# Feed-forward units of a hybrid decoder step: another order of factors and banks, and `down`'s low parts on GpSimd

## The chip, the cores and the metric

The kernel runs on one core of a Trainium2 chip. The time is device microseconds of that core, from one execution of the whole program; three runs of the kernel before are given by their median. Engines are named as in the profile: PE (TensorE, matmuls), PEld (its weight loads), DVE (VectorE), ACT (ScalarE), POOL (GpSimd), SP (SyncE, which only issues DMAs here).

## The reference, cut to what matters

One decoder layer for 1024 prompt tokens and 8 decode tokens (T = 1032 columns), model width 1024: a half-step feed-forward block, a mixer (windowed attention beside a Mamba-2 scan), cross attention, and a second half-step feed-forward block. The change touches the two feed-forward blocks:

```python
def swiglu(x, w_gate, w_up, w_down):
    return (jax.nn.silu(x @ w_gate) * (x @ w_up)) @ w_down
...
    x = x + (0.5 * swiglu(rms_norm(x, g_ffn1), w1_gate, w1_up, w1_down)).astype(x.dtype)
...
    x = x + (0.5 * swiglu(rms_norm(x, g_ffn2), w2_gate, w2_up, w2_down)).astype(x.dtype)
```

w_gate and w_up are 1024 x 2816, w_down is 2816 x 1024, all float32.

## The kernel before, in words

**Precision.** A float32 number is split into a high part (a cast to fp32r on ScalarE) and a low part (the difference, by a subtraction on DVE or GpSimd). A product is three matmuls: high x high, high x low, low x high (`three`, L328). Weights are split as they arrive by `split` (L315), which sends the low part to DVE and GpSimd in turn (L320); its high part is the cast at L319. Activations are split by `put` (cast L264, subtraction L265).

**Seven products for eight.** A unit works on 128 rows of the hidden width. The 1032 tokens are cut into P0 (388), P1 (388) and the rest R (256). For P0 and P1 a 2 x 2 block product is done in the Strassen-Winograd way: four weight matrices A11, A12, A21, A22 and four sums of them, S1 to S4 (`add_up`, the sum itself at L366), times the activation factors B11, B21, B22, T1 to T4, seven products in all, accumulated in three PSUM banks b1, b2, b3. The rest R is an ordinary product with the four A matrices, in a fourth bank.

**Units and pairs.** `gate_up(m)` loads 512 KB of gate and 512 KB of up weights (`raw_`, L325, two raw buffers for all units), makes the matrices, runs the products against the normalized x, and writes the hidden block with its own factors (`put`). Two `gate_up` units are followed by one `down`, which loads two blocks of 512 KB of w_down and adds its products to x (L501 to L518). There are 11 pairs in each block; the last `down` is `down_last`, an ordinary product. In unit 0 (`late`) the rest products come after all others.

**Banks.** Two sets of four PSUM banks are taken in turn by units; `down` runs twice (c = 0, 1) and uses both sets each time. In both kinds of unit b1 holds A11 x B11, a ScalarE copy seeds b2 from b1 (L399 in `gate_up`, L499 in `down`), and further products are accumulated on b2. Order of products in `gate_up`: A11, S2, A12, S3, S1, S4, A22, A21 (rest only). In `down`: A11, A21 (rest only), S1, S2, A12, S3, S4, A22.

**Weights in SBUF.** Split matrices live in four buffers (`fw`), raw weights in two (`fraw`), the sums in one tile (`fs`). Copies out of PSUM live in the ring `ts` of three buffers.

**Order.** The source order is a preference: the scheduler of the framework, which runs a timeline of its own, writes each engine's queue, and an engine then works through its queue in order. `mid1`, called after every `gate_up` of the first block, issues on SP a copy of 576 KB into u_scr for m = 4, 6, ..., 18, placed behind the load that `st["load"]` names at that time (L802).

Of the kernel before, what the change touches and what calls it, by code (L numbers as in the profile page):

```python
# [76 lines left out]
def tile_step(ctx, tc, a, o):  # L77
# [263 lines left out]
    def ffn(x, F, wg, wu, wd, fin, turn, mid=None):  # L341
# [27 lines left out]
        def gate_up(m):  # L369
            q = m % 2  # L370
            g_, u_ = raw_(cols_of(wg, m * 128)), raw_(cols_of(wu, m * 128))
            t = {"A11": g_[:, :512], "A12": g_[:, 512:], "A21": u_[:, :512], "A22": u_[:, 512:]}
            bk, rb = bank_set()
            b1, b2, b3 = bk
            sums = sums_of(m)
            e = {}

            def mat(name):
                if name == "S2":
                    add_up("S1", t, sums[:, :512])  # L380
                if name in SUMS and name not in t:
                    add_up(name, t, sums[:, :512] if name == "S3" else sums[:, 512:1024])
                return split(two(512), t[name])

            def rest(name, w):
                i = name in ("A21", "A22")
                first, last = name in ("A11", "A22"), name in ("A12", "A21")
                for j in range(4):
                    three(rb[:, int(i)], w, j, F["R"][j + (4 if name in ("A12", "A22") else 0)], first and j == 0, last and j == 3)

            def rest_end():
                gr, hr = u1_(NR), u1_(NR)
                nc.scalar.activation(gr, rb[:, 0], AF.Silu)
                nc.vector.scalar_tensor_tensor(hr, rb[:, 1], 0.5, gr, op0=OP.mult, op1=OP.mult)
                put(Hd["R"][q], hr, nc.vector)

            def evac(name):
                if name == "A11":
                    nc.scalar.copy(b2, b1)  # L399
                elif name == "S2":  # L400
                    e["U2"] = acc_(PA)
                    nc.scalar.copy(e["U2"], b2)
                elif name == "A12":
                    e["g0"] = g1_(PA)
                    nc.scalar.activation(e["g0"], b1, AF.Silu)
                elif name == "S3":
                    e["U3"] = acc_(PA)
                    nc.scalar.copy(e["U3"], b2)  # L408
                elif name == "S1":
                    e["u1"] = sq_(PA)  # L410
                    nc.vector.tensor_add(e["u1"], b3, e["U3"])  # L411
                elif name == "S4":
                    g1, u1 = g1_(PA), e["u1"]
                    nc.vector.tensor_add(g1, b3, e["U2"])
                    nc.scalar.activation(g1, g1, AF.Silu)
                    nc.vector.scalar_tensor_tensor(u1, u1, 0.5, g1, op0=OP.mult, op1=OP.mult)
                    if Hd["plain"]:
                        put(Hd["B22" if q else "B12"], u1, nc.vector)
                    elif q:
                        b12, t1 = Hd["b"]  # L420
# [1374 lines left out]
```

## Time and profile before

| | us |
|---|---|
| three runs, median (lowest, highest) | 2684.96 (2679.42, 2686.81) |
| profiled execution | 2680.7 |
| its span, first to last instruction | 2678.6 |
| PE busy | 2508.9 |
| DVE busy | 1806.0 |
| ACT busy | 1172.3 |
| POOL busy | 906.3 |

The first feed-forward block runs from about 105 to 831 us, the second from about 1940 to the end. An engine's busy time is the union of its instructions; a releaser is what an engine was waiting for when it stood idle, written as engine, tile and line.

### The profile page before, as it was taken

To read this page: it belongs to the slowest core of one execution; us is meant where nothing else is said; L and a number is where in the kernel's file an instruction comes from. 1 tells how busy PE (TensorE), PEld (TensorE's weight loads), DVE (VectorE), ACT (ScalarE), POOL (GpSimd) and SP (SyncE) were. 2 spreads that over 40 slices of the span, in tenths; PEclk is the share of its full clock that TensorE was granted. 3 is DMA by queue.
4 is the path that set the end of the run, shared out by engine and by line. 5 is a ranking of instruction groups with operands and counts; after the bars stand their busy time and mean duration, and the time that the engine had idled before them with its cause. 6 is when DMAs were issued, how large, how long until landed. Compare 5 with 4: busy or idle time off the path is not lost.

```text
span 2678.6 us, 42139 instructions
## 1 busy us (share of the span) xinstructions
PE 2508.9 (94%) x15999; PEld 2384.3 (89%) x15999; DVE 1806.0 (67%) x3660; ACT 1172.3 (44%) x2415; POOL 906.3 (34%) x675
## 2 busy tenths in 40 slices
PE   6899999999999999999797899989699999999998
PEld 5899999999998899999576899978689999999997
DVE  8566666666656777778568877564876666666665
ACT  5443333333334455554467623333343333333345
POOL 5433333333334111115156564102443333333333
PEclk9999999999999999999898999999899999999999
DMA  5411111111113222327657634573011111111112
GB/s 172 135 50 64 57 57 58 61 59 57 57 48 112 81 70 65 92 75 239 201 167 221 221 108 132 169 236 104 23 48 48 48 48 49 55 48 52 51 48 80
DMA packets 273747, 252.12 MB, mean 94 GB/s; under 512 B 17392, under 2 KB 243880, under 8 KB 273536
## 3 DMA queue, kind: packets, MB, share of 16 engines
q1 hardware_dynamic: 271872, 249.34, 30.2%
q8 instruction: 126, 2.06, 0.3%
q14 instruction: 77, 0.63, 0.1%
q10 hardware_dynamic: 1672, 0.09, 0.0%
HBM read 204.25 MB, written 49.98 MB: 95 GB/s over the span
## 4 chain that ended last, share of the span: by engine, by line
PE 70%; DVE 15%; DMA 7%; issue 3%; ACT 3%; POOL 1%; SPq 0%; DVEq 0%; ACTq 0%; POOLq 0%
PE fb L332 44%; PE pqkv L245 5%; PE pxbc L245 4%; PE pcq L245 3%; DMA fraw<-in_w_up_dram 2%; PE pco L245 2%; PE pwa L245 1%; DVE fs L366 1%; PE pwo L245 1%; PE po L1071 1%; PE ps L1045 1%; PE ptr L1065 1%; PE pd L245 1%; PE pzz L245 1%; PE cps L1604 1%
## 5 line engine op out<-in xcount | busy, mean ns | idle before, releaser
L235 POOL TENSOR_TENSOR wl<-wr,wh 128x1024 fp32r<-128x1024 f32 (+4 forms) x79 | 166.1, 2103 | 562.1 <-ACT wh L231 537.2
L320 POOL TENSOR_TENSOR fw<-fraw,fw 128x512 fp32r<-128x512 f32 x131 | 174.2, 1330 | 465.8 <-ACT fw L319 392.4
L320 POOL TENSOR_TENSOR fw<-fs,fw 128x512 fp32r<-128x512 f32 x128 | 172.3, 1346 | 400.4 <-ACT fw L319 347.2
L319 ACT CAST fw<-fs 128x512 fp32r<-128x512 f32 x256 | 158.2, 618 | 268.5 <-PE fb L332 152.5
L319 ACT CAST fw<-fraw 128x512 fp32r<-128x512 f32 x262 | 162.2, 619 | 189.6 <-PE fb L332 185.9
L366 DVE TENSOR_TENSOR fs<-fraw 128x512 f32<-128x512 f32 (+1 forms) x168 | 101.0, 601 | 141.7 <-DMA fraw<-in_w_up_dram 67.0
L320 DVE TENSOR_TENSOR fw<-fraw,fw 128x512 fp32r<-128x512 f32 x131 | 102.5, 782 | 110.9 <-ACT fw L319 110.6
L320 DVE TENSOR_TENSOR fw<-fs,fw 128x512 fp32r<-128x512 f32 x128 | 95.5, 746 | 99.1 <-ACT fw L319 99.1
L332 PE MATMUL fb<-hRh,fw 128*128 128x256 f32 x640 | 137.3, 280 | 0.5
L231 ACT CAST wh<-wr 128x1024 fp32r<-128x1024 f32 (+1 forms) x80 | 76.8, 960 | 99.4 <-PE pqkv L245 23.4
L332 PEld LDWEIGHTS fb<-hRh,fw 128*128 128x128 f32 x640 | 109.2, 188 | 3.7 <-DVE x L516 3.7
L245 PE MATMUL pxbc<-xh,wh 128*128 128x344 f32 x288 | 94.0, 326 | 2.0 <-DVE xr L882 2.0
L245 PE MATMUL pqkv<-xh,wh 128*128 128x344 f32 x288 | 94.0, 326 | 0.4 <-DVE x L546 0.3
L245 PE MATMUL pxbc<-xl,wh 128*128 128x344 f32 x288 | 93.5, 324 | 0.0
L245 PE MATMUL pqkv<-xh,wl 128*128 128x344 f32 x288 | 93.1, 323 | 0.0
L245 PE MATMUL pqkv<-xl,wh 128*128 128x344 f32 x288 | 93.0, 323 | 0.0
L245 PE MATMUL pxbc<-xh,wl 128*128 128x344 f32 x288 | 92.9, 323 | 0.0
L332 PE MATMUL fb<-hRl,fw 128*128 128x256 f32 x320 | 87.6, 278 | 0.0
L411 DVE TENSOR_TENSOR tu<-fb,ts 128x388 f32<-128x388 f32 x44 | 24.7, 562 | 90.3 <-ACT ts L408 90.3
L1052 ACT ACTIVATE pr<-pr,nm 128x128 f32<-128x128 f32 (+3 forms) x64 | 49.7, 776 | 53.7 <-DVE nm L1050 53.3
L332 PE MATMUL fb<-T2h,fw 128*128 128x388 f32 x160 | 53.8, 357 | 17.1 <-ACT fb L499 17.1
L245 PE MATMUL pzz<-xh,wh 128*128 128x344 f32 x192 | 64.3, 335 | 4.1 <-DVE tv L914 2.2
(798 smaller groups left out, 9395.8 us busy)
## 6 DMA issues: line engine op xcount, KB each, us to landing
fraw<-in_w_gate_dram SPq DMA_DIRECT2D x44, 512.0 KB
fraw<-in_w_up_dram SPq DMA_DIRECT2D x44, 512.0 KB
fraw<-in_w_down_dram SPq DMA_DIRECT2D x44, 512.0 KB
wr<-in_w_in_dram SPq DMA_DIRECT2D x32, 512.0 KB
x_scr<-x SPq DMA_DIRECT2D x16, 516.0 KB
x<-x_scr SPq DMA_DIRECT2D x16, 516.0 KB
bc<-acs_scr SPq DMA_DIRECT2D x16, 512.0 KB
ckv<-in_cache_mem_k_dram SPq DMA_DIRECT2D x16, 512.0 KB
```

Source lines behind the costliest of these rows:

```text
L231: nc.scalar.copy(hi[:, :w], raw[:, :w])
L235: e.tensor_sub(lo[:, q], raw[:, q], hi[:, q].bitcast(F32))
L245: nc.tensor.matmul(ps, w, v, start=i == 0, stop=i == last)
L319: nc.scalar.copy(hi, src)
L320: (nc.vector if st["turn"] else nc.gpsimd).tensor_sub(lo, src, hi.bitcast(F32))
L332: nc.tensor.matmul(ps, l[:, js], m, start=bool(start and not i), stop=bool(stop and i == 2), skip_group_check=True)
L366: nc.vector.tensor_tensor(dst, t[p], t[q], op=op)
L1045: ins = nc.tensor.matmul(ps[:, c:c + n], qs[:, b * 128:w], kk[:, c:c + n], start=i == 0, stop=i == 1)
L1052: nc.scalar.activation(pr[:, :w], pr[:, :w], AF.Exp, scale=-1.0, bias=nm, accum_out=sm)
L1065: nc.tensor.transpose(p[:, j], pr[:, (c + j) * 128:(c + j + 1) * 128], ident)
L1071: nc.tensor.matmul(po[:, b % 2].rearrange("p i t -> p (i t)"), vv[:, j, e].rearrange("p i d -> p (i d)"), tts[j // 4][:, j % 4].rearrange( ...
L1604: nc.tensor.matmul(ps[:, u], l_[:, d, tk], r_[:, d], start=i == 0, stop=i == 5)
```

## The change

`gate_up` and `down` no longer issue instructions themselves. Each returns a list of slots: a function that makes the slot's weights, one that issues its products, and a chain of evacuations. `run` walks through the slots of the whole block, asks for the weights of slot i+1 before it issues the products of slot i (AHEAD = 1), and issues the first link of a slot's evacuations after its products and each further link one slot later. `mid(m)` is called after the last slot of a unit.

`gate_up`: the order becomes A11, A12, S2, S1, S3, S4, A21, A22. The seed copy still goes from b1 to b2. The product with T1 is copied out of b3 (`s1`) before S3 is evacuated, instead of S3 being copied (`U3`). In A21 and A22 the rest product precedes the other.

`down`: the order becomes A11 and A21, S1 and S2, S4 and S3, A12 and A22, four slots per c. All four sums are made together. The low parts of all eight matrices go to GpSimd. The result of A12 is copied out of PSUM by ScalarE and added to x by GpSimd (`moved`); it was one DVE addition.

Matmuls and loads are the same in number and shape. The diff, cut to its core:

```diff
-    def split(hl, src, like=lambda t: t):
+    def split(hl, src, like=lambda t: t, eng=None):
         hi, lo = like(hl[0]), like(hl[1])
-        st["turn"] = not st.get("turn")
+        if not eng:
+            st["turn"] = not st.get("turn")
+            eng = nc.vector if st["turn"] else nc.gpsimd
         nc.scalar.copy(hi, src)
-        (nc.vector if st["turn"] else nc.gpsimd).tensor_sub(lo, src, hi.bitcast(F32))
+        eng.tensor_sub(lo, src, hi.bitcast(F32))
...
-    ORDER = (("A11", 0, "B11", True), ("S2", 1, "T2", False), ("A12", 0, "B21", False), ("S3", 1, "T3", False),
-             ("S1", 2, "T1", True), ("S4", 2, "B22", False), ("A22", 1, "T4", False), ("A21", None, None, False))
...
+            def product(name, b, f, first, late):
+                def mm(w):
+                    if not e:
+                        e["bk"], e["rb"] = bank_set()
+                    if name in ("A21", "A22") and not late:
+                        rest(name, w)
+                    if f:
+                        for j in range(4):
+                            three(e["bk"][b], w, j, F[f][j], first and j == 0, j == 3)
+                    if name in ("A11", "A12") and not late:
+                        rest(name, w)
+                return mm
...
+            for name, b, f, first, evs in (
+                    ("A11", 0, "B11", True, (seed,)), ("A12", 0, "B21", False, (silu,)), ("S2", 1, "T2", False, (kept("U2", 1),)),
+                    ("S1", 2, "T1", True, (kept("s1", 2),)), ("S3", 1, "T3", False, (up1,)), ("S4", 2, "B22", False, (gate1, hid1, hid1b)),
+                    ("A21", None, None, False, ()), ("A22", 1, "T4", False, (hid0 if late else ends, hid0b))):
...
+                def mats(names, c=c, t=t):
...
+                    if names[0] in SUMS:
+                        i = 0 if names[0] == "S1" else 2
+                        for j, nm in enumerate(() if i else ("S1", "S2", "S3", "S4")):
+                            add_up(nm, t, t["sums"][:, j * 256:(j + 1) * 256])
+                        hl = split(two(512), t["sums"][:, i * 256:(i + 2) * 256], eng=nc.gpsimd)
                     else:
+                        hl = split(two(512), t["wa" if names[0] == "A11" else "wb"], twice, eng=nc.gpsimd)
...
+                def moved(x_, b):
+                    t_ = acc_(PA)
+                    nc.scalar.copy(t_, b)
+                    nc.gpsimd.tensor_add(x_, x_, t_)
...
+                    for e in U:
+                        three(e["b"][0], W[0], e["j"], Hd["B11"], True, True)
+                        nc.scalar.copy(e["b"][1], e["b"][0])
...
+                def sums12(W, U=U):
+                    for i, b, f, r_ in ((0, 2, "T1", 1), (1, 1, "T2", 0)):
+                        for e in U:
+                            three(e["b"][b], W[i], e["j"], Hd[f], i == 0, True)
+                            add(e["x"][r_][:, P1], e["b"][b])
...
+                    for i, b, f, r_ in ((1, 2, "B22", 0), (0, 1, "T3", 1)):
...
+                for names, mm in ((("A11", "A21"), first), (("S1", "S2"), sums12), (("S3", "S4"), sums34), (("A12", "A22"), final)):
+                    out.append((lambda names=names, mats=mats: mats(names), mm, ()))
...
+            for i in range(-AHEAD, len(slots)):
+                if i + AHEAD < len(slots):
+                    W[i + AHEAD] = slots[i + AHEAD][0]()
...
+                mm(W.pop(i))
+                todo, left = left, []
+                for evs_ in todo + [evs]:
+                    if evs_:
+                        evs_[0]()
+                        left.append(evs_[1:])
+                if after:
+                    after()
```

## Rows read from the trace of the kernel before

**Rows 1.** The page's table of engines: busy us (share of the span) x instructions.
```profile
PE 2508.9 (94%) x15999; PEld 2384.3 (89%) x15999; DVE 1806.0 (67%) x3660; ACT 1172.3 (44%) x2415; POOL 906.3 (34%) x675
```

**Rows 2.** Busy time by stretch: PE, PEld, DVE, ACT, POOL; granted clock; DMA share, GB/s.
```profile
170.70:753.30 582.60, 566.13 (x3565) 559.45 (x3565) 369.65 (x712) 224.28 (x442) 182.02 (x145) 0.99 0.19 58
...
2008.60:2584.00 575.40, 569.45 (x3568) 554.28 (x3568) 376.91 (x713) 225.31 (x443) 186.29 (x145) 1.00 0.17 50
```

**Rows 3.** Waits of PE, four stretches in time order: us in total, times, longest.
```profile
PE fb L332 <- ACT fb L399: 2.9, 1, 2.9
...
PE fb L332 <- ACT fb L499: 17.1, 10, 2.7
...
PE fb L332 <- ACT fb L399: 3.5, 1, 3.5
...
PE fb L332 <- DVE x L507: 4.8, 9, 0.5
```

**Rows 4.** Timelines of SP, POOL, DVE, ACT, PE, 228 to 235: start, us, instruction, [idle before].
```profile
228.13 0.38 SPq L325 DMA_DIRECT2D fraw<-in_w_up_dram  x1
228.56 0.58 SPq L802 DMA_DIRECT2D u_scr<-r_scr  x1
...
232.13 1.28 POOL L320 TENSOR_TENSOR fw<-fraw,fw 128x512 fp32r<-128x512 f32 x1 [3.04 <-issue]
...
232.49 1.47 DVE L366 TENSOR_TENSOR fs<-fraw 128x512 f32<-128x512 f32 x1 [0.94 <-DMA fraw<-in_w_up_dram]
233.88 1.01 DVE L511 TENSOR_TENSOR x<-x,fb 128x388 f32<-128x388 f32 x2
...
234.46 0.93 ACT L499 COPY fb<-fb 128x388 f32<-128x388 f32 x2 [2.46 <-DVE x L511]
...
234.98 0.44 PE L332 MATMUL fb<-T2h,fw 128*128 128x388 f32 x1 [1.86 <-ACT fb L499]
```

**Rows 5.** Timelines of DVE and PE, 169 to 171, a pair without a copy into u_scr.
```profile
169.01 0.69 DVE L366 TENSOR_TENSOR fs<-fraw 128x512 f32<-128x512 f32 x1 [0.53 <-DMA fraw<-in_w_up_dram]
...
170.72 0.45 PE L332 MATMUL fb<-T2h,fw 128*128 128x388 f32 x1 [0.68 <-ACT fb L499]
```

**Rows 6.** Busy time by stretch, as in rows 2, of 3.4 us each.
```profile
299.40:302.80 3.40, 3.40 (x14) 3.40 (x14) 2.58 (x6) 0.23 (x1) 0.00 (x0) 0.51 0.00 0
302.90:306.30 3.40, 3.40 (x22) 3.40 (x22) 2.24 (x5) 0.62 (x1) 0.00 (x0) 1.00 0.00 0
...
623.70:627.10 3.40, 3.40 (x13) 3.40 (x14) 2.66 (x6) 0.31 (x1) 0.00 (x0) 0.50 0.00 0
...
1948.10:1951.50 3.40, 3.40 (x11) 3.40 (x12) 3.40 (x6) 1.65 (x4) 1.67 (x2) 0.50 0.00 0
```

**Rows 7.** Timeline of PE: the first of twelve matmuls, and what follows them.
```profile
304.92 0.34 PE L332 MATMUL fb<-B110h,fw 128*128 128x388 f32 x1
...
307.04 0.34 PE L332 MATMUL fb<-T3h,fw 128*128 128x388 f32 x1
```

**Rows 8.** Busy time by stretch, second block: most of a `down`, then gate/up.
```profile
2184.00:2200.30 16.30, 15.64 (x98) 14.06 (x96) 15.79 (x33) 6.74 (x15) 7.38 (x6) 1.00 0.21 61
2200.30:2247.90 47.60, 47.60 (x301) 47.50 (x302) 25.92 (x48) 18.26 (x37) 13.31 (x11) 1.00 0.15 46
```

**Rows 9.** Groups by line and shape: count | busy us, mean ns of one | idle before.
```profile
L320 POOL TENSOR_TENSOR fw<-fraw,fw 128x512 fp32r<-128x512 f32 x131 | 174.2, 1330 | 465.8 <-ACT fw L319 392.4 <-DVE fs L366 31.0 <-issue 30.0
...
L320 DVE TENSOR_TENSOR fw<-fraw,fw 128x512 fp32r<-128x512 f32 x131 | 102.5, 782 | 110.9 <-ACT fw L319 110.6
...
L511 DVE TENSOR_TENSOR x<-x,fb 128x388 f32<-128x388 f32 x80 | 42.3, 552 | 4.8 <-PE fb L332 4.8
...
L402 ACT COPY ts<-fb 128x388 f32<-128x388 f32 x44 | 21.3, 484 | 70.2 <-PE fb L332 70.2
...
L265 POOL TENSOR_TENSOR T4l<-tu,T4h 128x388 fp32r<-128x388 f32 x20 | 20.6, 1030 | 0.0
```

**Rows 10.** Timeline of ACT at the start of the first block.
```profile
110.22 0.62 ACT L319 CAST fw<-fs 128x512 fp32r<-128x512 f32 x1 [2.88 <-DVE fs L366]
110.75 0.61 ACT L319 CAST fw<-fraw 128x512 fp32r<-128x512 f32 x1
```

More of the change, by code (lines that the diff above doesn't have):

```diff
@@ L370, in gate_up @@
             q = m % 2
[L371 to L376, printed above, removed]
-            def mat(name):
[L379 to L382, printed above, removed]
+            t, e, out = {}, {}, []
+            def mat(name):
+                if not t:
+                    g_, u_ = raw_(cols_of(wg, m * 128)), raw_(cols_of(wu, m * 128))
+                    t.update(A11=g_[:, :512], A12=g_[:, 512:], A21=u_[:, :512], A22=u_[:, 512:], sums=sums_of(m))
+                if name in SUMS:
+                    sums = t["sums"]
+                    for nm in {"S2": ("S1", "S2"), "S1": ()}.get(name, (name,)):
+                        add_up(nm, t, sums[:, :512] if nm in ("S1", "S3") else sums[:, 512:1024])
                 return split(two(512), t[name])
@@ L386, in rest @@
                 i = name in ("A21", "A22")
-                first, last = name in ("A11", "A22"), name in ("A12", "A21")
+                first, last = name in ("A11", "A21"), name in ("A12", "A22")
                 for j in range(4):
-                    three(rb[:, int(i)], w, j, F["R"][j + (4 if name in ("A12", "A22") else 0)], first and j == 0, last and j == 3)
-            def rest_end():
[L392 to L395, printed above, removed]
@@ new lines, in rest @@
+                    three(e["rb"][:, int(i)], w, j, F["R"][j + (4 if name in ("A12", "A22") else 0)], first and j == 0, last and j == 3)
+            def product(name, b, f, first, late):
[10 more added lines that the diff above has]
+                return mm
@@ new lines, in hid1b, with hid0 @@
+            def hid1b():
+                if q and not Hd["plain"]:
+                    b12, u1 = Hd["b"][0], e["u1"]
+                    put(Hd["B22"], u1, nc.gpsimd)
+                    nc.vector.tensor_sub(b12, u1, b12)
+                    put(Hd["T3"], b12, nc.gpsimd)
+            def hid0():
+                u0 = e["u0"] = sq_(PA)
+                nc.vector.scalar_tensor_tensor(u0, e["bk"][1], 0.5, e["g0"], op0=OP.mult, op1=OP.mult)
+                put(Hd["B21" if q else "B11"], u0, nc.vector)
@@ L444, in gate_up @@
                 if late and name == "A21":
                     continue
-                if name == "S3":
-                    early["S1"] = mat("S1")
-                w = early.pop(name, None) or mat(name)
-                if f:
-                    for j in range(4):
-                        three(bk[b], w, j, F[f][j], first and j == 0, j == 3)
-                if f:
-                    evac(name)
-                if name[0] == "A" and not late:
-                    rest(name, w)
+                out.append((lambda name=name: mat(name), product(name, b, f, first, late), evs))
@@ L549, in ffn, with hidden @@
         last = DFF // 128 - 2
-        for m in range(0, DFF // 128, 2):
+        def hidden(m):
             for nm in MATS if m < last else ("B11", "B12", "B21", "B22"):
@@ L554, in ffn @@
             Hd["plain"] = m == last
+        units = []
+        for m in range(0, DFF // 128, 2):
             for i in range(2):
-                with nullcontext():
-                    gate_up(m + i)
-                if mid:
-                    mid(m + i)
+                units.append(((lambda m=m: hidden(m)) if not i else None, lambda m=m + i: gate_up(m),
+                              (lambda m=m + i: mid(m)) if mid else None))
             if m < last:
-                with nullcontext():
-                    down(m)
-            else:
-                turn()
-                down_last(m)
+                units.append((None, lambda m=m: down(m), None))
+        E_ = mybir.EngineType
+        with nullcontext():
+            run(units)
+        turn()
+        down_last(last)
     x_scr = dp.tile([DM, T], F32, name="x_scr")
```

208 lines of the change are left out of this document (101 added, 107 removed).

## The prediction

> **What bounds the kernel now.** I read the table of busy times first, then the waits of PE by stretch, then the timelines of the other engines around the longest waits. TensorE (PE) is busy for 94% of the span and its weight loads for 89% [rows 1]: the kernel is bound by the matrix engine, and only time in which PE stands still or runs slowly can be won. In the steady part of each feed-forward block PE is busy for 566.1 of 582.6 us (first) and 569.5 of 575.4 us (second) [rows 2]. So the change, which touches these blocks alone, works on about 16 + 6 us of idle time and on the slow clock behind it. The waits of PE tell where that time is [rows 3]: in the first block it is one wait, ten times, 17.1 us in all, for the ScalarE copy at L499 (the seed of bank 2 in `down`); in the second it is a wait of 0.53 us for the addition at L507. Each block also begins with one wait for the seed copy at L399, of 2.9 and 3.5 us.
>
> The reader is to see in [rows 4] how the long wait arises. The load of the next unit's up weights leaves at 228.13 us and the copy into u_scr that `mid1` issues sits right behind it. VectorE (DVE) runs its queue in order; the sum at L366 (S1 of the next gate/up unit) is ahead of the last additions of the first half (c = 0) of `down` (L511), and waits 0.94 us for that load. When it starts it meets the GpSimd subtraction of 1.28 us and takes 1.47 us. L511 follows, then the seed copies of the second half (c = 1), then PE, 1.86 us late. Where no copy is behind the load, the DVE wait is 0.53 us, the sum 0.69 us, and PE is 0.68 us late [rows 5]. So the u_scr copy costs about 1.2 us in eight of ten pairs of units (m = 4 to 18).
>
> After three of these waits the granted clock was 0.50 to 0.51 for 3.4 us, which is the 1.2 GHz level; before the fall PE had stood idle as in [rows 4], and right behind the stretch it is 1.00, 2.4 GHz ([rows 6]: the first and the last of the three, what follows the first, and the one at the start of the second block). In 3.4 us at half clock 1.7 us of work are lost. The same follows the starting waits.
>
> **The change part by part.**
>
> *No work of PE is added.* Per pair of units there are 264 matmuls in gate/up and 132 in `down`, before and after. Only their order and banks differ.
>
> *The copy into u_scr moves.* `st["load"]` is now read when the first matrix of unit m+1 has been asked for, since matrices are requested one slot ahead. The eight copies thus go behind the up load of the odd unit, on SP's queue, not behind that of the even unit that follows a `down`. Behind them on SP stand only the `down` loads, which come several slots later. In gate/up DVE has room (25.9 of 47.6 us busy, against 15.8 of 16.3 us in the stretch with `down` [rows 8]), so I cost the copy there at nothing; without that room it is the 1.2 us of before in eight pairs, 9.6 us. What then sets the handover is what it is in the second block, 0.53 us. The sum: 17.1 us now, 10 x 0.53 = 5.3 us after, **-11.8 us**. The three slow-clock stretches behind waits of 1.9 us go: 3 x 1.7, **-5.1 us**. Bounds: nothing gained (the wait moves to another place), or all 17.1 + 5.1.
>
> *Gate/up order A11, A12, S2, S1, S3, S4, A21, A22.* The second product no longer reads a seeded bank. In unit 0, where A11 has no rest product behind it, A12 x B21 now fills the wait: 12 matmuls of 388 columns start in 2.12 us [rows 7]. Of 2.89 us in the first block the gate weights of A12 were there all along, its cast being only queued behind the sum [rows 10]. In the second, B21 comes from the same step as B11. So 2.1 us twice, **-4.2 us**, and I take half of the two dips of clock, **-1.7 us**. Bounds 0 and 2 x (2.9 + 1.7) = 9.2 us.
>
> *End of a block.* A21, whose rest product used to stand behind A22, now precedes it. The hidden block from A22 is wanted by `down_last`, whose products on B11 can run meanwhile: cost nothing; uncovered it is 12 matmuls of 256 columns, at most 2.1 us per block by the wider ones of [rows 7].
>
> *Down: low parts and four additions go to GpSimd.* Four of the eight subtractions of a `down` leave DVE (0.78 us each) and arrive at GpSimd at 1.33 us; four additions at L503 leave DVE (0.55 us) and become a ScalarE copy (0.48 us, by the copies at L402) and a GpSimd addition, not seen in this shape there; nearest is L265 T4l at 1.03 us (the same 388 columns, two SBUF inputs), and I take it [rows 9]. DVE: -4 x 0.78 - 4 x 0.55 = -5.3 us per `down`. GpSimd: 4 x 1.33 + 4 x 1.03 = +9.4 us. ScalarE: +1.9 us, and it has 9.6 of 16.3 us free [rows 8]. In the stretch where DVE was at 97%, GpSimd goes from 7.4 to 16.8 of 16.3 us [rows 8]: it changes places with DVE as the tightest engine there. What hides it: `down` lasts 84 x 0.177 + 48 x 0.12 = 20.6 us on PE (0.12 us for 256 columns is scaled from the 388), the first subtraction can be done before it, and four weight buffers allow it to run ahead. If a low part is late, PE waits at the third matmul of that product; if an addition is late, the three `ts` buffers are full, the next ScalarE copy stands still, and the casts behind it on ScalarE with it, and then PE.
>
> *A shorter distance between bank uses.* In `down` S1 and S4 share bank 3 with one product pair (6 matmuls, 1.06 us) between, S2 and S3 bank 2 likewise. The addition between takes 0.55 us on DVE, if DVE is free when the product ends. Together with GpSimd's lateness I bound this new cost by 0 (all hidden, as 9.4 us of 20.6 are free) and by 2.8 us per `down` (the slow rival below), and take 0.3 us, nearer to the free end, since the scheduler can put other products between as it does now: 20 x 0.3 = **+6 us**. The 0.53 us waits of the second block I leave as they are: DVE gains 5.3 us there but loses some to GpSimd.
>
> **The sum.** -11.8 - 5.1 - 4.2 - 1.7 + 6 = -16.8 us. The profiled execution took 2680.7 us (span 2678.6 and 2.1 around it), which gives 2663.9. The median of the three runs is 4.3 us above it; I add half of that: 2666 us.
>
> **What GpSimd does to DVE.** The rows show it: a sum with two SBUF inputs took 0.69 us alone and 1.47 us when a GpSimd subtraction was under way [rows 4, 5], while L511, which reads PSUM and SBUF, never took over 0.56 us [rows 9]. The Trainium skill, "SBUF — State Buffer", section "Who interferes with whom", states the rule: a DVE instruction with two SBUF inputs and a GpSimd instruction that reads SBUF share a read interface, and whoever starts first keeps it for the whole instruction. By that rule the change would slow the sums and subtractions of DVE in a `down` and not its additions to x, which is the slow rival below; the trace agrees for L366 and L511.
>
> **The rivals.**
> *Slow: DVE is held up by GpSimd.* In a `down` DVE has 13 instructions with two SBUF inputs (8 sums, T2l, B21l, 3 differences). If each waits half a GpSimd instruction of 1.33 us, DVE does 15.8 - 5.3 + 13 x 0.66 = 19.1 us of work in a stretch of 16.3, and PE waits 2.8 us per `down`: +56 us, against 22.8 us gained: 2714 us. It decides from 1.14 us per `down` on (22.8 / 20). For it: GpSimd at 16.8 of 16.3 us. Against it: gate/up leaves DVE half free, where such work can go. At 2 us per `down` the time is 2698.
> *No change.* The handover wait only moves: DVE's queue is still in order, and the scheduler may again put a sum that waits for a load ahead of an addition that PE needs, at 0.5 us more per pair than I take. Then 2681 + 2 us or so. For it: the order of PE now is already mixed by the scheduler, so the new order in the source is only a preference; that the written order is not what runs is part of this case.
> *All stalls go.* Handovers in both blocks, starts and dips: 17.1 + 5.1 + 5.3 + 9.2 = 36.7 us, and no new cost: 2644 us.
>
> **How the numbers follow.** Forecast 0.50 (2655 to 2676), no change 0.22, slow 0.18, all stalls 0.10. Runs of this kernel lie within 0.3% (2679 to 2687), so 8 us is what counts: faster is below 2677, which takes the forecast and the fast rival, 0.60; same 0.22; slower above 2693, 0.18. The range goes from 2646, next to the fast rival, to 2698, the slow rival at 2 us per `down`.
>
> **What would show it.** Right: the waits of PE for L499's successor in the first block fall to 0.5 us each, no DVE sum waits for the up load with x additions behind it, the u_scr copies stand behind odd units' loads, the clock stays at 1.00 from the start to the last unit, the first wait of each block is under 1.5 us. GpSimd's busy time rises by about 190 us, DVE's falls by about 100. Wrong: waits of PE on GpSimd's `fw`, on x additions, or sums with a mean well over 0.42 us in `down`, twenty times.

## The result and the profile after

The kernel after took 2703.52 us (median of five runs, 2701.48 to 2712.03) beside 2684.96 us for the kernel before: a ratio of 1.0081, interval 1.0065 to 1.0097 (the two medians alone give 1.0069). It is 0.8% slower where 0.7% faster was forecast, and lies above the range. The profiled execution took 2703.5 us, span 2701.7.

The page's table of engines, after (answers to [rows 1]):

```profile
span 2701.7 us, 42378 instructions
...
PE 2511.2 (93%) x15999; PEld 2386.9 (88%) x15999; DVE 1804.3 (67%) x3500; ACT 1199.3 (44%) x2495; POOL 1109.1 (41%) x835
```

DVE has 160 instructions less and the same busy time, where a fall of about 100 us was expected. GpSimd has 203 us more, as expected (190). From the first product on a block's banks (one without weights, some time ahead of unit 0) to the last, the first block went from 703.6 to 713.5 us and the second from 714.0 to 730.3; everything else together is 3.2 us shorter. Nine pairs of units by stretch (columns as in [rows 2]):

```profile
151.80:745.90 594.10, 569.47 (x3566) 559.96 (x3565) 371.17 (x640) 236.77 (x478) 274.80 (x217) 0.99 0.18 57
2000.40:2588.70 588.30, 568.30 (x3565) 557.26 (x3564) 374.57 (x639) 235.77 (x476) 274.95 (x216) 0.99 0.16 49
```

PE's idle time in them is 24.6 and 20.0 us, against 16.5 and 6.0 in [rows 2]. The waits of PE say where it is (first block, then second; answers to [rows 3]):

```profile
PE fb L334 <- DVE hRl L265: 17.0, 10, 1.9
PE fb L334 <- DVE x L509: 10.3, 30, 0.6
PE fb L334 <- ACT fb L410: 1.9, 1, 1.9
...
PE fb L334 <- DVE hRl L265: 12.1, 10, 1.2
PE fb L334 <- DVE T2l L265: 7.1, 10, 0.7
PE fb L334 <- ACT fb L410: 3.7, 2, 3.5
PE fb L334 <- DVE x L509: 2.4, 11, 0.3
```

The handover wait of [rows 3] inside `down` (L499, 17.1 us) is gone. In its place PE waits for DVE. Most of it, 36.2 us, comes early in a `down`, for hRl and T2l, which the unit before it has to write (the rest rows R and the factor T2 of the hidden block). Of the additions to x, the 10.3 us of the first block come where `down` ends, 23 to 28 us after its first product; the kernel before has no such wait there. The passage from gate/up to `down` is thus the first place to look at. PE before, around one passage of the second block (timeline: start, us, instruction):

```profile
2178.85 0.29 PE L332 MATMUL fb<-R3h,fw 128*128 128x256 f32 x1
2178.97 0.34 PE L332 MATMUL fb<-T40h,fw 128*128 128x388 f32 x1
...
2180.21 0.34 PE L332 MATMUL fb<-B220h,fw 128*128 128x388 f32 x1
...
2183.21 0.34 PE L332 MATMUL fb<-B11h,fw 128*128 128x388 f32 x1
```

The last of 24 rest products (R0 to R7) is followed by 24 products on T4 and B22, and only then comes `down` (B11). After, the same passage:

```profile
2188.54 0.28 PE L334 MATMUL fb<-R3l,fw 128*128 128x256 f32 x1
2188.66 0.34 PE L334 MATMUL fb<-B220h,fw 128*128 128x388 f32 x1
...
2192.21 0.28 PE L334 MATMUL fb<-R7h,fw 128*128 128x256 f32 x1
2192.33 0.34 PE L334 MATMUL fb<-T40h,fw 128*128 128x388 f32 x1
...
2194.45 0.34 PE L334 MATMUL fb<-B11h,fw 128*128 128x388 f32 x1
...
2199.51 0.45 PE L334 MATMUL fb<-T2l,fw 128*128 128x388 f32 x1 [0.71 <-DVE T2l L265]
...
2201.34 0.50 PE L334 MATMUL fb<-hRl,fw 128*128 128x256 f32 x2 [1.20 <-DVE hRl L265]
```

Eleven rest products stand ahead of S4 x B22 and thirteen behind it (in the first block two and twenty-two). They end 2.0 us before `down` begins, not 4.1. DVE before, and then after, in the same passage:

```profile
2179.93 0.42 DVE L394 SCALAR_TENSOR_TENSOR tv<-fb,tv 128x256 f32<-128x256 f32 x1
...
2181.05 0.42 DVE L265 TENSOR_TENSOR hRl<-tv,hRh 128x256 fp32r<-128x256 f32 x1
2182.53 0.56 DVE L414 TENSOR_TENSOR tg<-fb,ts 128x388 f32<-128x388 f32 x1 [1.06 <-PE fb L332]
...
2186.32 0.56 DVE L421 TENSOR_TENSOR tu<-tu 128x388 f32<-128x388 f32 x1
2186.80 0.56 DVE L424 TENSOR_TENSOR tu<-tu 128x388 f32<-128x388 f32 x1
```

```profile
2191.40 0.43 DVE L364 TENSOR_TENSOR fs<-fraw 128x256 f32<-128x256 f32 x1 [3.22 <-DMA fraw<-in_w_down_dram]
2191.75 0.56 DVE L428 TENSOR_TENSOR tg<-fb,ts 128x388 f32<-128x388 f32 x1
...
2193.60 1.56 DVE L438 TENSOR_TENSOR tu<-tu 128x388 f32<-128x388 f32 x1
2195.09 1.65 DVE L445 TENSOR_TENSOR tu<-tu 128x388 f32<-128x388 f32 x1
2196.65 0.41 DVE L404 SCALAR_TENSOR_TENSOR tv<-fb,tv 128x256 f32<-128x256 f32 x1
...
2197.83 1.63 DVE L265 TENSOR_TENSOR T2l<-tu,T2h 128x388 fp32r<-128x388 f32 x1
...
2200.87 0.41 DVE L265 TENSOR_TENSOR hRl<-tv,hRh 128x256 fp32r<-128x256 f32 x1
```

Before, R is multiplied and split (L394, hRl) while DVE has room: it is done at 2181.5, 1.7 us before `down`, and DVE then idles. After, the results of S4 (L428, L438, L445) stand ahead of R's (L404); the first sum of `down` has waited 3.22 us for a load, with these behind it; and L438, L445 and T2l take 1.56 to 1.65 us where L421 and L424 took 0.56 and T2l 0.90. Over the ten passages of each block, L445 takes 1.66 and 1.65 us (L424 0.55 and 0.56 before) and T2l 1.38 and 1.64 (0.55 and 0.91); L438 is long in the second block only (1.56, in the first 0.56). hRl is done at 2201.3, 6.8 us after `down` began. Over the ten passages of a block the median of hRl's end, against the first product of `down`, went from -1.1 to +5.6 us in the first block and from -1.8 to +6.7 in the second. The load does not explain the first block: DVE waits 0.5 us for it there (median), 2.1 before. In the second it waits 3.0 us, 1.5 before, which can be part of the lateness. GpSimd meanwhile, after:

```profile
2193.45 2.86 POOL L322 TENSOR_TENSOR fw<-fs,fw 128x512 fp32r<-128x512 f32 x2 [3.90 <-ACT fw L321]
2196.27 1.35 POOL L265 TENSOR_TENSOR B22l<-tu,B22h 128x388 fp32r<-128x388 f32 x1
2197.58 1.46 POOL L322 TENSOR_TENSOR fw<-fraw,fw 128x512 fp32r<-128x512 f32 x1
```

It runs without a pause over just the stretch in which DVE's subtractions take three times their time. Two groups by line and shape, after (columns as in [rows 9]), the moved addition and a sum for the gate/up units:

```profile
L515 POOL TENSOR_TENSOR x<-x,ts 128x388 f32<-128x388 f32 x80 | 88.6, 1129 | 15.4 <-ACT ts L514 15.4
L364 DVE TENSOR_TENSOR fs<-fraw 128x512 f32<-128x512 f32 x88 | 71.7, 815 | 65.7 <-DMA fraw<-in_w_up_dram 62.7 <-POOL x L515 1.8 <-POOL fw L322 1.2
```

The moved addition takes 1.13 us (1.03 was put), so GpSimd's price was nearly right. The sums of one shape, 0.69 us where alone ([rows 5]), are 0.82 us on average, but they were 0.77 before as well.

### The profile page after: what moved, and what is told of

It is laid out like the page before. It is cut to its first block, busy times and chain, and to the rows that moved or that the text cites. A ratio compares the mean times of both kernels' runs of the same rounds, so it can differ in the third digit from the quotient of the medians.

```text
span 2701.7 us, 42378 instructions
## 1 busy us (share of the span) xinstructions
PE 2511.2 (93%) x15999; PEld 2386.9 (88%) x15999; DVE 1804.3 (67%) x3500; ACT 1199.3 (44%) x2495; POOL 1109.1 (41%) x835
## 5 line engine op out<-in xcount | busy, mean ns | idle before, releaser
L322 POOL TENSOR_TENSOR fw<-fs,fw 128x512 fp32r<-128x512 f32 x168 | 230.6, 1377 | 372.7 <-ACT fw L321 355.3
L322 POOL TENSOR_TENSOR fw<-fraw,fw 128x512 fp32r<-128x512 f32 x171 | 230.1, 1346 | 321.0 <-ACT fw L321 321.0
L509 DVE TENSOR_TENSOR x<-x,fb 128x388 f32<-128x388 f32 (+1 forms) x560 | 258.7, 510 | 44.8 <-PE fb L334 42.4
L364 DVE TENSOR_TENSOR fs<-fraw 128x512 f32<-128x512 f32 (+1 forms) x168 | 117.9, 702 | 140.4 <-DMA fraw<-in_w_up_dram 62.7
L322 DVE TENSOR_TENSOR fw<-fraw,fw 128x512 fp32r<-128x512 f32 x91 | 70.7, 777 | 133.4 <-ACT fw L321 132.8
L322 DVE TENSOR_TENSOR fw<-fs,fw 128x512 fp32r<-128x512 f32 x88 | 61.4, 698 | 94.1 <-ACT fw L321 94.1
L334 PE MATMUL fb<-hRl,fw 128*128 128x256 f32 x320 | 87.6, 288 | 29.1 <-DVE hRl L265 29.1
L515 POOL TENSOR_TENSOR x<-x,ts 128x388 f32<-128x388 f32 x80 | 88.6, 1129 | 15.4 <-ACT ts L514 15.4
L334 PEld LDWEIGHTS fb<-hRl,fw 128*128 128x128 f32 x320 | 58.9, 189 | 34.3 <-DVE hRl L265 34.3
L415 ACT COPY ts<-fb 128x388 f32<-128x388 f32 x88 | 42.5, 483 | 85.4 <-PE fb L334 85.4
```

Source lines behind the costliest of these rows:

```text
L322: eng.tensor_sub(lo, src, hi.bitcast(F32))
L364: nc.vector.tensor_tensor(dst, t[p], t[q], op=op)
L415: nc.scalar.copy(e[name], e["bk"][b])
L509: nc.vector.tensor_add(x_, x_, b)
L515: nc.gpsimd.tensor_add(x_, x_, t_)
```

## The experiments

Two theories at first. **Load** (theory G in some expectations): GpSimd's added work holds DVE's instructions that read two operands from SBUF, so the relief of DVE comes back as longer instructions and PE waits. **Order** (theory O): the queues that the scheduler writes for the new order make DVE late where PE needs it, whoever does the low parts. This table holds all kernels; what follows is read against it. Each ratio is to the kernel before as it ran beside that kernel, 2675 to 2677 us (median) in the experiments; the times in us of the expectations start from 2685. F1 and F2 are the first and second block as above, us, of the profiled execution; idle is PE's in both, ahead of their products; gate/up and `down` are the old or the new units; low: all low parts of `down` on GpSimd; add: A12's addition on GpSimd; copy: the copies into u_scr behind the odd units.

```
kernel     ratio   F1     F2     idle  gate/up down low add copy
before     1       703.6  714.0  33.5  old     old  -   -   -
e2_pool    0.9977  703.2  707.1  33.1  old     old  yes -   -
e3_copy    0.9958  689.6  713.4  23.7  old     old  -   -   yes
e10_moved  0.9932  692.7  711.8  27.4  old     old  -   yes -
e11_best   0.9966  704.6  709.4  34.9  old     old  yes -   yes
e13_copy_mv 0.9932 691.3  709.1  26.7  old     old  -   yes yes
e15_all_old 0.9968 703.5  704.9  35.5  old     old  yes yes yes
e16_down_o. 0.9918 683.1  715.2  22.8  old     new  -   -   -
e19_new_end 0.9916 682.4  713.5  22.2  old, end edited; else as e16
e6_down    1.0127  695.4  751.1  52.1  old     new  yes yes -
e5_gate    1.0039  716.2  718.4  49.7  new     old  -   -   -
e12_order  1.0040  711.3  724.4  53.5  new     new  -   -   yes
e1_turns   1.0041  701.5  730.5  47.2  new     new  -   yes yes
e7_add     1.0037  703.4  728.5  48.8  new     new  yes -   yes
after      1.0081  713.5  730.3  58.3  new     new  yes yes yes
e8_now     1.0069  714.5  729.8  57.1  as after, evacuations at once
e9_final   1.0182  726.8  740.2  60.3  as after, R's products later
e17_products 1.0091 717.9 729.3  59.9  as after, old order of products
e18_old_end 1.0212 746.7  733.2  83.5  as after, old end of gate/up
```

The half-widths of the intervals are 0.0013 to 0.0026; e4_pinned (1.0536, F1 762.9, F2 797.5) is left out. The stage between the blocks, which no edit touches, took 1106 to 1118 us in these executions; so a block is compared by F1 and F2, a kernel by its ratio. F2 begins some 23 us ahead of unit 0, and in that stretch PE waits 14 to 18 us for a step that no edit touches, so a difference of 4 us between two F2 says little.

### Parts of the change in the old order

```diff
# e2_pool, split() with eng; then in down:
-  hi, lo = split(two(512), src, ...)
+  hi, lo = split(two(512), src, ..., eng=nc.gpsimd)
# e3_copy, in mid1:
-  if m >= 4 and m % 2 == 0 and m < 20:
+  if m >= 5 and m % 2 == 1 and m < 20:
# e10_moved, in down:
-  add(xa[:, P0], xa[:, P0], b1)
+  t_ = acc_(PA)
+  nc.scalar.copy(t_, b1)
+  nc.gpsimd.tensor_add(xa[:, P0], xa[:, P0], t_)
# e11_best = e2 + e3;  e13_copy_mv = e3 + e10;  e15_all_old = e2 + e3 + e10
```

**e2_pool.** 

> The kernel before, with one part of the change: all low parts of down on GpSimd. Theory G: 0.5 to 1 us more per pair, 2695 to 2705 us, with new waits of PE on DVE low parts or sums at the passage from gate/up to down. Theory O: DVE is relieved and nothing waits, 2680 to 2688 us.

Measured: 0.9977 [0.9963, 0.9990]. The low parts on GpSimd do no harm in the old order, although the time of DVE's SBUF instructions above their shortest (0.55 us for 388 elements, 0.42 for 256, 0.69 for 512) rose from 2.0 to 4.5 us per pair in the first block.

**e3_copy.** 

> The kernel before, with the eight copies into u_scr issued behind the up load of the odd unit (m = 5 to 19) and not behind that of the even one. By the prediction's own term the wait for L499 falls from 1.87 to about 0.7 us in eight pairs and the slow-clock stretches behind it go: 10 to 15 us less, 2670 to 2676 us. Rival: the wait is set by the load alone and the copy does nothing: 2685 us.

Measured: 0.9958 [0.9941, 0.9975]; F1 falls by 14.0 us, F2 is the same. PE's wait for L499 is 8.3 us in all (17.1 before), and the three clock stretches behind it are gone: the copy was the cause of half of that wait and of the slow clock.

**e10_moved.** 

> The kernel before, and of the change only the moved addition: in a down unit A12's result is copied out of PSUM by ACT and added to x by GpSimd, where DVE adds it out of PSUM. Theory 1 (GpSimd holds up DVE's additions that read two SBUF operands, so work taken off DVE comes back in its other instructions): ratio 1.002 to 1.004, DVE's busy time falls by less than half of the 0.6 us per unit taken off. Theory 2 (DVE is relieved): ratio 0.998 to 1.000. Theory 3 (its cost in the kernel after came of the queue order there): within 0.3% of before.

Measured: 0.9932 [0.9913, 0.9951]: better than any of the three theories. The L499 wait is gone here too, with the copies where they were, and 10.0 us for L520 stand in its place. How one addition less on DVE lets the seed copy start in time was not followed further. Both parts of the load, one by one, are gains.

**e11_best, e13_copy_mv.** 

> The kernel before with the copies into u_scr behind the odd units and all low parts of the down units on GpSimd: the two parts that were faster by themselves (0.9958 and 0.9977). If their gains add: 0.993 to 0.995, some 16 us less. If the second's gain was the first's (both take away part of the same handover waits): 0.996, no better than the copies alone. If GpSimd's lateness shows once the handover is gone: over 0.997.

> The kernel before with two parts of the change: the copies into u_scr behind the odd units, and A12's result copied out by ACT and added by GpSimd (0.9958 and 0.9932 by themselves). If both gains add: 0.988 to 0.990. If both only take away the same waits of FFN1 (17.1 us, and three dips of 1.7): about 0.992 to 0.994, as the moved addition alone.

Measured: 0.9966 [0.9951, 0.9981] and 0.9932 [0.9917, 0.9947]. Nothing adds: each part takes away the same wait, and with the low parts another comes (13.5 us of L509 in the first block of e11).

**e15_all_old.** 

> The kernel before with all that the change moves to another engine or place (the low parts of the down units and A12's addition on GpSimd, the copies behind the odd units), in the old order of products and sums. Theory 1 (the order is what loses; the load on GpSimd is harmless): 0.990 to 0.997, and DVE's and GpSimd's busy times are those of the kernel after within 15 us. Theory 2 (the load loses as soon as both parts of it stand together): 1.003 to 1.008, with DVE's excess over its lone durations at 6 to 7 us per pair of units as after.

Measured: 0.9968 [0.9953, 0.9982]: theory 1. The page's table has the instructions of the kernel after, and GpSimd's busy time within 13 us of it, but not DVE's:

```profile
PE 2500.3 (94%) x15999; PEld 2378.3 (89%) x15999; DVE 1767.3 (66%) x3500; ACT 1201.8 (45%) x2495; POOL 1096.7 (41%) x835
```

DVE is 37 us below the kernel after. The same work, in the old order, is 1.1% faster than in the new: the load alone is not the loss. It is not free either: beside e13, which lacks only the low parts, e15 is 0.4% slower.

### The new units, one kind at a time

```diff
# e5_gate: the kernel before with the new gate_up, each unit by itself
-  gate_up(m + i)
+  run([(None, lambda m=m + i: gate_up(m), None)])
# e6_down: the kernel before with the new down
-  down(m)
+  run([(None, lambda m=m: down(m), None)])
# e16_down_order = e6; e12_order = the kernel after; in both
-  hl = split(two(512), ..., eng=nc.gpsimd)
+  hl = split(two(512), ...)
-  moved(e["x"][0][:, P0], e["b"][0])
+  add(e["x"][0][:, P0], e["b"][0])
```

**e5_gate.** 

> The kernel before with the new gate/up alone (its slots, order and links of evacuations, run unit by unit), the old down and the copy into u_scr where it was. Theory A (the new gate/up ends with the rest product and A22, so that hRl, T2l and B21l come due together at the passage to down): slower than before by 10 to 25 us, with waits for hRl or T2l. Theory B (the new down, whose sums share banks at half the distance, is the cost): within 5 us of before. Theory C (only both together cost): within 5 us of before.

Measured: 1.0039 [1.0024, 1.0054], F1 716.2, F2 718.4: theory A by its time, but hardly by its waits (hRl 0.8 us, T2l 5.8). PE's queue up to the first product of `down` is that of the kernel after, and hRl comes 4.1 and 5.8 us after the first product of `down` (median, first and second block). No work is moved and the copies stay, yet PE waits for additions to x, early in a `down`, and for weight parts on DVE:

```profile
PE fb L332 <- DVE x L533: 12.4, 10, 1.3
PE fb L332 <- DVE fw L320: 8.4, 10, 1.0
```

**e6_down.** 

> The kernel before with the new down alone (its order and banks, all low parts and the moved additions on GpSimd). Theory A: not slower than before, 0 to 10 us faster as with the low parts alone. Theory B: slower by 10 to 25 us with waits for the additions to x. Theory C: within 5 us of before.

Measured: 1.0127 [1.0110, 1.0144]. This is more than theory B put, and by other waits. The first block gains 8 us, the second loses 37. The clock falls in seven of the ten `down` there. Two waits of PE make most of its idle time: for the cast of T2 early in `down` and, behind `down`, for the seed copy of the next unit. ScalarE waits for DVE before both (before one T2h 2.17 us, before the copies of L401 26.9 us in all):

```profile
PE fb L334 <- ACT T2h L264: 17.9, 10, 2.5
...
PE fb L334 <- ACT fb L401: 12.3, 11, 3.7
```

**e16_down_order.** 

> The kernel before with the down units of the change, but their low parts in turn on DVE and GpSimd and A12's addition on DVE: of the change only the order of the down unit's products, sums and weight parts, and the banks. Theory 1 (this order is the loss): 1.004 to 1.013, near the 1.0127 of the new down units with their load, and TensorE waits for the additions to x, which free a bank that the next product but one wants, 0.8 us or more per down unit. Theory 2 (order and load only together): within 0.3% of before.

Measured: 0.9918 [0.9899, 0.9938]. Theory 1 falls by its sign: the new order of `down` is the best part of the change. PE's waits in F1, but for the start, are gone; in F2 two are left:

```profile
PE fb L334 <- DVE x L487: 5.6, 10, 0.6
PE fb L334 <- ACT T2h L264: 4.7, 10, 0.5
```

The distance of 0.8% from before is outside theory 2 as well. So the load, which in the old `down` changed little (e15 beside e3, 0.1%), costs 2.1% in the new one (e16 to e6).

**e12_order.** 

> The kernel after with the low parts of the down units in turn on DVE and GpSimd, and A12's result added by DVE out of PSUM: what is left of the change is the other order of factors and banks, the slots, the copies behind the odd units and the order left to the scheduler. Theory 1 (all that the change lost came of the load on GpSimd): 0.996 to 1.000, as the copies alone give. Theory 2 (the order and the banks lose by themselves): 1.003 to 1.006, with waits for DVE's parts in FFN2.

Measured: 1.0040 [1.0024, 1.0056]: theory 2. Beside e16 it has the new gate/up units, the requests that run on from unit to unit and the moved copies, and is 1.2% slower. PE's waits, first and second block:

```profile
PE fb L334 <- DVE x L509: 18.7, 30, 1.7
...
PE fb L334 <- DVE x L509: 15.3, 10, 1.6
```

### The kernel after with one thing changed

```diff
# e1_turns: as the split() lines of e12_order; e7_add: as its moved() line
# e8_now, in run():
-  for evs_ in todo + [evs]: ... evs_[0](); left.append(evs_[1:])
+  for ev in evs:
+      ev()
# e4_pinned, around run(units)
-  with nullcontext():
+  with tc.manual_schedule(engines={E_.PE, E_.DVE, E_.Activation, E_.Pool}):
# e9_final, in final(), around the products on R[1]:
+  with tc.issue_after(st["mm"]):    # the last product of sums34
# e17_products: slots first, sums12, A12's half of final, sums34 + A22's half
# e18_old_end, in gate_up:
-  ("A21", None, None, False, ()), ("A22", 1, "T4", False, (ends, hid0b))
+  ("A22", 1, "T4", False, (hid0, hid0b)), ("A21", None, None, False, (rest_end, rest_end2))
   # and A22's rest product behind its product on T4
# e19_new_end: e16_down_order with the opposite edit of ORDER and rest
```

**e1_turns, e7_add.** 

> The changed kernel, but the low parts of down alternate between DVE and GpSimd again. Theory G (GpSimd low parts hold up DVE's instructions with two SBUF inputs at the passage from gate/up to down, so hRl and T2l come late): the waits for hRl (1.2 to 1.9 us a pair) and T2l (0.7 us) fall under 0.5 us and L438, L445 and T2l go back to about 0.6 us each; 2680 to 2688 us. Theory O (the new order of slots and evacuations is what makes hRl late, whoever makes the low parts): the waits stay, 2698 to 2704 us.

> The changed kernel with the result of A12 added to x by DVE again, without the ScalarE copy and the GpSimd addition. If the moved additions are part of the cost by GpSimd's load: 5 to 10 us less than the changed kernel (ratio to before 1.004 to 1.006). If they are hidden: the ratio of the changed kernel, 1.008, or more, since DVE gets 2 us of work per down back.

Measured: 1.0041 [1.0026, 1.0056] and 1.0037 [1.0024, 1.0050]. Either half of the load taken back gives 0.4%; both taken back (e12) give no more. The hRl waits go with the low parts (1.1 us left in the first block) and stay without the addition (17.8). For e1 neither theory holds whole: its ratio lies between the two, L445 is back at 0.55 us in the first block, T2l is not (1.05 and 1.62), and PE waits for x (9.5 and 16.1 us).

**e8_now, e4_pinned.** 

> The changed kernel with all links of a slot's evacuations issued right after its products instead of one slot later each. If the later place in the source makes hRl and T2l late: the waits shrink and the ratio falls to 1.000 to 1.004. If the scheduler puts them by readiness anyway: 1.007 to 1.009.

> The changed kernel, with PE, DVE, ACT and POOL kept in the order of the source inside the feed-forward units. Theory O in a narrower form (the scheduler puts products with hR of the second unit ahead of T2 and sums that wait for a load ahead of hRl): the two waits vanish, 2660 to 2690 us. Theory G: GpSimd's share is the same and the waits stay or grow, 2700 us or more.

Measured: 1.0069 [1.0054, 1.0084], the deferred evacuations are not it; and 1.0536 [1.0521, 1.0552]: the written order, run as written, is far worse than the scheduler's, with waits of PE for weight parts.

**e9_final.** 

> The kernel after, with one link more: the products of the unit's last part (the ones that read the high part hR) are queued on TensorE behind the last product of sums34, where after the scheduler put two of them ahead of the rest of T2. Theory 1 (the place in TensorE's queue turns a late DVE into a wait): the waits for hRl, 17.0 us in FFN1 and 12.1 in FFN2, fall under 8 us together, and no other wait grows by as much; ratio 0.997 to 1.002. Theory 2 (DVE is late whatever stands next): the same time is waited for T2l, B22 or the x additions, or comes back in the unit's end, and the ratio stays at 1.006 to 1.010.

Measured: 1.0182 [1.0156, 1.0207]; theory 1 falls. The hRl waits are gone, and others of their size are there:

```profile
PE fb L334 <- ACT fb L523: 14.2, 10, 1.6
PE fb L334 <- DVE x L509: 12.5, 20, 0.8
```

hRl comes as late as after (+5.6 and +6.5 us): DVE is late, and PE waits for whatever comes next. The ratio is above theory 2's as well. PE's idle time is that of the kernel after (60.3 to 58.3 us); the other loss is the clock, told below.

**e17_products.** 

> The kernel after with one edit: A12 x B21 and its rest product stand between the products of S1, S2 and those of S3, S4, as before, so that a bank has six products or more between its uses and the pair A12, A22 is asked for one slot earlier. Theory 1 (the short way between two uses of a bank is the loss): 0.993 to 1.000, and TensorE's waits in the two blocks fall by 10 us or more each. Theory 2 (DVE is late at the passage from gate/up to down whatever stands next): 1.005 to 1.010, with the waits for hRl or what takes its place still over 20 us in all.

Measured: 1.0091 [1.0076, 1.0106]: theory 2. The way between two uses of a bank is not what makes the loss.

**e18_old_end, e19_new_end.** 

> The kernel after with the end of its gate/up units as before: A22's product on T4, its rest product, then A21's rest product, and the low part of R behind that. Theory 1 (the end of gate/up is the loss): hRl is written before the down unit's first product again, the waits for hRl (17.0 and 12.1 us) are gone and nothing of their size takes their place; ratio 0.992 to 1.000. Theory 2 (each queue order has its own waits and no single edit decides): the waits for hRl go but others come, ratio 1.004 to 1.010. Theory 3 (the new down units with their load on GpSimd lose whatever stands ahead of them, as in the kernel with the new down units alone): 1.010 to 1.014, with waits for T2 in FFN2.

> The kernel before with the order of the new down units (0.9918 so far), and the end of the gate/up units as in the change: A21's and A22's rest products ahead of A22's product on T4. Theory 1 (the end is the loss): 1.000 to 1.006, hRl written 4 us or more after the down unit's first product, and waits of TensorE for hRl or for parts behind it on DVE's queue of 10 us or more in each block. Theory 2: within 0.3% of 0.9918, and the lateness of hRl costs nothing since its products can stand later.

Measured: 1.0212 [1.0190, 1.0234] and 0.9916 [0.9894, 0.9938]: neither is what theory 1 said, and e19 has theory 2's number without being a test of it. The timelines tell why. In e18, first block, PE and then DVE:

```profile
218.45 0.28 PE L334 MATMUL fb<-R0h,fw 128*128 128x256 f32 x1
...
219.87 0.34 PE L334 MATMUL fb<-B11h,fw 128*128 128x388 f32 x1
...
226.45 0.49 PE L334 MATMUL fb<-hRh,fw 128*128 128x256 f32 x1 [3.58 <-DVE tv L402]
```

```profile
225.98 0.41 DVE L402 SCALAR_TENSOR_TENSOR tv<-fb,tv 128x256 f32<-128x256 f32 x1
```

The edit, meant to bring R forward, put twelve rest products (ten in the second block) at the very end of the unit; R is late by 3 us more than after, and PE waits 35.5 and 14.7 us for it (17.0 and 12.1 after). In e19, second block, PE:

```profile
2149.22 0.34 PE L334 MATMUL fb<-T40h,fw 128*128 128x388 f32 x1
...
2153.47 0.34 PE L334 MATMUL fb<-B11h,fw 128*128 128x388 f32 x1
```

That is the order of the kernel before: T4 and B22 behind all rest products, 4.25 us ahead of `down`. The source was changed and the queue was not, so the time is that of e16. (The rest products had been ahead of T4 in the queue of before, though the source had them behind.) Neither kernel undoes what it was to undo; what they do show is that the later the rest products run, the longer PE waits for R, in three steps within one structure of `down`: in the first block none with their end at -4.1 us against the first product of `down` (e6, e16, e19), 17.0 us at -2.0 (after), 35.5 at +0.2 (e18). The rest products are not all of it: they end at -2.0 in e5, e12 and e1 too, where the low parts are not all on GpSimd, and there PE waits 0.8, 0.5 and 1.1 us for hRl.

## Why the prediction was wrong

**What bounds the kernel: right.** All of the loss is PE's idle time and slow clock in the two blocks.

**The copy into u_scr, -11.8 and -5.1: right by itself, somewhat too large.** e3 has it alone: F1 -14.0 us, by the ratio -11 us. In the kernel after the L499 wait is gone as forecast, but in the same block 10.3 us of waits for x have come at the end of `down`, where 5.3 us were put for all that is left at the handover.

**Unit 0, -4.2 and -1.7: the first wrong, 1 us came; the second right by luck.** Of the two dips of clock that of the first block is gone, which is the half that was put, but in six of the eight other kernels with the new gate/up it is there. The starting wait is 1.9 and 3.5 us (2.9 and 3.5 in [rows 3]), and the waiting product is A12 x B21 itself: it accumulates on b1, which the seed copy (L410) has first to read. I had looked at the bank that is seeded and not at the bank that is read.

**Order of gate/up and its end, costed at nothing: the step that failed.** I priced the move of A21's rest product at the end of a block, and the new order in unit 0 alone; the ten passages to `down` in each block I left as they were. There the queue of after has twenty-two (first block) or thirteen rest products behind S4 x B22, and R comes 6.7 and 8.5 us later against the first product of `down`. The wait for hRl alone is 29.1 us. The new gate/up units cost 0.4% with nothing else of the change (e5) and 1.2% ahead of the new `down` without its load (e12 beside e16, with the moved copies and the requests that run on). All nine kernels of the table that have them are slower than before, and in each hRl ends 4 us or more after the first product of `down` (median of a block); of the nine others only e6 is slower, and in all of them hRl ends, by the same median, before that product. Counted from unit 0's first product, the second block takes 695 us or more in the nine, and 693 or less in the others but e6 (728).

**GpSimd's lateness and the bank distance, +6: the distance cost less by itself, and both together more.** In e16, which has the new distances and the old gate/up, PE waits 5.6 us for additions to x, all in the second block, where the kernel before waits 5.3; new are 4.7 us for T2h. With the new gate/up in front (e12) the waits for x are 34.0 us, 1.7 per `down`.

**DVE -5.3, GpSimd +9.4 per `down`: half right.** Per pair, over nine pairs of each block, first and second:

```
          DVE busy     GpSimd busy   DVE above its shortest times
before    41.1  41.8   20.2  20.7    2.0  3.1
after     41.3  41.6   30.5  30.6    6.6  7.2
e15       39.5  39.0   29.4  30.2    4.7  4.5
e12       43.1  46.3   20.2  20.5    4.5  7.4
e16       40.9  42.6   20.2  20.8    1.9  3.6
```

GpSimd got its 10 us. DVE's relief was paid back, 4.6 and 4.1 us in longer instructions. That is the mechanism of the slow rival, with about half of the 8.6 us (13 x 0.66) it put, and the forecast of that rival, 2714, is nearer than mine. But e15 shows that the load does not decide by itself, and e12 that the order lengthens DVE's work with no load moved (T2l 1.05 and 1.64 us there and in e5, 0.55 and 0.91 before). The prediction had taken order and load as two terms of a sum; from e3 on (0.9958), the new order costs 0.8% and the load in it another 0.4% (e12, after), while in the old order the load costs 0.1% in sum (e15: the addition by itself gains, e13, and the low parts lose it again), and behind the old gate/up the new `down` gains 0.8% without it and loses 1.3% with it.

**What stays open.** Which line of the new gate/up makes the scheduler put S4 x B22 among the rest products (A12 second, S1 ahead of S3, or the requests one slot ahead) was not isolated, and e5 has all of them; the edit of the end went the other way (e18). That R's lateness causes the hRl wait rests on the timelines and on the three steps, not on a kernel that undoes it; in e12 hRl is late as well (+4.5 and +6.3 us), and PE waits for x instead.

The versions that beat both kernels are e16 and e19, 2652 to 2655 us: the new order of `down`, and nothing else of the change.

## What to carry to other kernels

Cost a new order at each place where it recurs, from the queue that runs and not from the source: ask behind which product each result that the next unit needs now stands, and what is ahead of it on DVE. Where a scheduler writes the queues, parts of a change neither add nor keep their sign, so run each part by itself and with its neighbours (here 0.9918 and 1.0127 for one `down`), and look whether an edit changed the queue at all before reading its time. Work taken off an engine is a relief only if the engine that takes it does not hold it up.

## What the runs showed of the hardware

DVE's subtractions on 388 columns with two SBUF operands took 0.56 us (L421, L424 before) and 1.56 to 1.65 us with GpSimd working without a pause; the additions to x, which read PSUM, kept 0.55 us on average (400 of them). The Trainium skill, "SBUF — State Buffer", section "Who interferes with whom", says that such a DVE instruction contends with a GpSimd instruction that reads SBUF, and that whoever is first holds the shared ports for the whole instruction; the trace agrees, 0.56 us plus up to 1.1 us of a 1.3 to 1.4 us instruction.

The clock was the surprise. In e9 PE is idle for about as long as after, and its longest wait at a passage of the first block is shorter (1.6 us, after 1.9), yet the granted clock fell eleven times in that block, at the start and at each of the ten passages to `down`; after, only twice. Each passage of e9 has a wait of 1.3 to 1.6 us for L523 and then, with under 1 us of products between, one of 0.8 us for L509, and the clock falls within 0.5 us of the end of that wait or of a third. The second passage, PE's first two waits and then the stretch (columns as in [rows 6]):

```profile
223.21 0.45 PE L334 MATMUL fb<-T2h,fw 128*128 128x388 f32 x1 [1.37 <-ACT fb L523]
...
224.83 0.45 PE L334 MATMUL fb<-B22h,fw 128*128 128x388 f32 x1 [0.82 <-DVE x L509]
```

```profile
226.90:230.30 3.40, 3.40 (x12) 3.40 (x11) 2.42 (x5) 0.68 (x3) 2.07 (x3) 0.50 0.51 151
```

At 0.50, the 1.2 GHz level, PE did 12 products in 3.4 us, against 22 at full clock in [rows 6]. After, each passage of the first block has one wait of 1.6 to 1.9 us for hRl, and in eight of ten the clock stays. The number of waits alone does not tell: in the first block of e18 each passage has a single long wait, of 3.4 to 3.8 us, and the clock falls in all ten, while in the second block after each has two, of 0.7 and 1.2 us, and it falls in three. No run was made to tell more.
